# Instance normalisation: tiles of one row per partition in twelve buffers instead of two rows in six

## The chip, the cores and the metric

The kernel runs on one core of one Trainium2 chip. The metric is the device time of one execution in microseconds, from the first to the last instruction, as the median of several runs. The engines that matter are VectorE (DVE in the profile), which computes statistics, ScalarE (ACT), which applies a scale and a bias to every element and also issues the stores, SyncE (SP), which issues the loads, and the core's 16 DMA engines, which carry both.

## The reference

The input is 256 x 256 rows of 4096 floats (1073.74 MB), and the output has the same size. Each row is normalised by its own mean and variance.

```python
def setup_inputs():
    batch, channels, length = 256, 256, 4096
    return {"x": np.random.randn(batch, channels, length).astype(np.float32),
            "eps": np.float32(1e-5)}

def reference(x, eps):
    mean = np.mean(x, axis=2, keepdims=True)
    var = np.var(x, axis=2, keepdims=True)
    return ((x - mean) / np.sqrt(var + eps)).astype(np.float32)
```

All data must be read once and written once; a row of 16 KB fits into one partition of on-chip memory.

## The kernel before

A tile is 128 partitions x 2 rows x 4096 floats, 4 MB, so there are 256 tiles. Each partition's two rows lie next to each other in memory, 32 KB in one piece. Six such tiles fit at once. For every tile, SyncE issues the load. VectorE computes partial statistics of 512 elements each (eight per row), combines them (`bn_aggr`) to mean and variance. ScalarE takes the square root, VectorE the reciprocal and the bias -mean x rstd. ScalarE then normalises each row in place and issues the store from the same buffer.

```python
    P = 128
    K = 2
    BUFS = 6
    # ...
    x_t = x_flat.rearrange("(t p k) d -> t p k d", p=P, k=K)
    out_t = out_flat.rearrange("(t p k) d -> t p k d", p=P, k=K)
    # ... nsub = 8
    io = ctx.enter_context(tc.tile_pool(name="io", bufs=BUFS))
    small = ctx.enter_context(tc.tile_pool(name="small", bufs=2 * BUFS))
    # ...
    for i in range(ntiles):
        x_tile = io.tile([P, K, d], mybir.dt.float32)
        nc.sync.dma_start(out=x_tile, in_=x_t[i])

        # ... stats, mv, rstd, nbias from the small pool
        for r in range(K):
            for j in range(nsub):
                nc.vector.bn_stats(out=stats[:, r, j, :], in_=xr[:, r, j, :])
            nc.vector.bn_aggr(out=mv[:, r, :], in_=stats[:, r])

        nc.scalar.activation(out=rstd, in_=mv[:, :, 1], func=Sqrt, bias=eps_tile, scale=1.0)  # shortened
        nc.vector.reciprocal(out=rstd, in_=rstd)
        nc.vector.scalar_tensor_tensor(out=nbias, in0=mv[:, :, 0], scalar=-1.0, in1=rstd, ...)

        for r in range(K):
            nc.scalar.activation(out=x_tile[:, r, :], in_=x_tile[:, r, :], func=Identity,
                                 bias=nbias[:, r : r + 1], scale=rstd[:, r : r + 1])  # shortened
        nc.scalar.dma_start(out=out_t[i], in_=x_tile)
```

The order in which an engine executes is not that of the source. When the program is built, a scheduler decides for each engine in which order its instructions stand, and inserts the waits; on the chip every engine then works strictly in that order. The pools give out buffers in turn: a load into a buffer waits until the store that last read it has landed.

Of the kernel before, what the change touches and what calls it, by code (L numbers as in the profile page):

```python
# [1 line left out]

# [4 lines left out]


@with_exitstack  # L10
def kernel(
    ctx: ExitStack,
    tc: tile.TileContext,
    x: bass.AP,
    eps: bass.AP,
    out: bass.AP,
):
    nc = tc.nc
    P = 128
    K = 2  # L20
    BUFS = 6

    x_flat = x.flatten_outer_dims()
    out_flat = out.flatten_outer_dims()
    n, d = x_flat.shape
    rows_per_tile = P * K
    assert n % rows_per_tile == 0
    ntiles = n // rows_per_tile

    x_t = x_flat.rearrange("(t p k) d -> t p k d", p=P, k=K)  # L30
    out_t = out_flat.rearrange("(t p k) d -> t p k d", p=P, k=K)

    BN_FMAX = nc.vector.BN_STATS_FMAX
    nsub = (d + BN_FMAX - 1) // BN_FMAX
    assert d % BN_FMAX == 0

    io = ctx.enter_context(tc.tile_pool(name="io", bufs=BUFS))
    small = ctx.enter_context(tc.tile_pool(name="small", bufs=2 * BUFS))
    singles = ctx.enter_context(tc.tile_pool(name="singles", bufs=1))

    eps_tile = singles.tile([P, 1], mybir.dt.float32)
    nc.vector.memset(eps_tile, eps)  # L42

    for i in range(ntiles):
        x_tile = io.tile([P, K, d], mybir.dt.float32)
        nc.sync.dma_start(out=x_tile, in_=x_t[i])  # L46

        stats = small.tile([P, K, nsub, 6], mybir.dt.float32)
        mv = small.tile([P, K, 2], mybir.dt.float32)
        rstd = small.tile([P, K], mybir.dt.float32)  # L50
        nbias = small.tile([P, K], mybir.dt.float32)
        xr = x_tile.rearrange("p k (s f) -> p k s f", s=nsub)
        for r in range(K):
            for j in range(nsub):
                nc.vector.bn_stats(out=stats[:, r, j, :], in_=xr[:, r, j, :])  # L55
            nc.vector.bn_aggr(out=mv[:, r, :], in_=stats[:, r])  # L56

        nc.scalar.activation(  # L58
            out=rstd,
            in_=mv[:, :, 1],  # L60
            func=mybir.ActivationFunctionType.Sqrt,
            bias=eps_tile,
            scale=1.0,
        )
        nc.vector.reciprocal(out=rstd, in_=rstd)  # L65

        nc.vector.scalar_tensor_tensor(  # L67
            out=nbias,
            in0=mv[:, :, 0],
            scalar=-1.0,  # L70
            in1=rstd,
            op0=mybir.AluOpType.mult,
            op1=mybir.AluOpType.mult,
        )

        for r in range(K):
            nc.scalar.activation(  # L77
                out=x_tile[:, r, :],
                in_=x_tile[:, r, :],
                func=mybir.ActivationFunctionType.Identity,  # L80
                bias=nbias[:, r : r + 1],
                scale=rstd[:, r : r + 1],
            )
        nc.scalar.dma_start(out=out_t[i], in_=x_tile)


# [1 line left out]
_INS = ['x', 'eps']  # L88
_OUTS = [((256, 256, 4096), 'float32')]
#: Inputs that are plain numbers.  # L90
_NUMBERS = {'eps': 9.999999747378752e-06}


# [26 lines left out]
```

## Time and profile before

| | |
|---|---|
| time, median of 3 | 5180.87 us (5179.3 to 5187.54) |
| read + written | 1073.74 MB + 1073.74 MB |
| VectorE: partial statistics | 4096 of 674 ns, 2464.1 us |
| VectorE: combining | 512 of 363 ns, 185.7 us |
| ScalarE: normalising a row | 512 of 3793 ns, 1917.8 us |
| ScalarE: square root | 256 of 280 ns, 71.7 us |
| VectorE: reciprocal, bias | 256 each, 27.7 and 41.0 us |
| loads | 256 of 4096 KB, median 23.7 us from issue to landing |
| stores | 256 of 4096 KB, median 18.6 us from issue to landing |

The profile page gives each engine's busy time; its table of queues says how much of the 16 DMA engines' time the packets of each queue took. A further view lists who waited for whom; there the queue of SyncE (SPq) shows what each load had to wait for before it was issued. The chain that ended last goes back from the last instruction, at each step to what released it. Windows give busy time and moved bytes of a stretch. Below the page, the trace holds a record of every DMA packet with its start, duration, size and queue.

### The profile page before, as it was taken

How to read it: one execution, taken by the hardware profiler on the slowest of the kernel's cores; microseconds unless marked ns; L12 is line 12 of the kernel's file. 1: busy time of each engine (PE TensorE's matmuls, PEld its weight loads, DVE VectorE, ACT ScalarE, POOL GpSimd, SP SyncE). 2: the span in 40 equal slices, each digit the busy share in tenths (PEclk: the TensorE clock that was granted, in tenths of full speed). 3: DMA queues.
4: the chain of work that ended last, by engine and by line, in shares of the span. 5: the costliest groups of instructions: out<-in, count | busy, mean ns of one | idle time of the engine just before them, and what ended most of it. 6: DMA issues, size and time to landing. Idle time of an engine off the chain costs nothing.

```text
span 5180.7 us, 7450 instructions
## 1 busy us (share of the span) xinstructions
DVE 2654.0 (51%) x5121; ACT 1967.0 (38%) x769; POOL 0.2 (0%) x4
## 2 busy tenths in 40 slices
DVE  6544555554455555444555554455555445555543
ACT  3333333433333433433343433333343333334334
POOL 0000000000000000000000000000000000000000
DMA  9999999999999999999999999999999999999998
GB/s 425 412 410 413 420 417 422 417 414 416 410 416 413 417 418 414 413 412 417 417 416 418 413 414 418 410 417 420 417 415 417 417 413 417 417 419 415 415 416 367
DMA packets 73786, 2147.99 MB, mean 415 GB/s; under 512 B 8192, under 2 KB 8192, under 8 KB 8192
## 3 DMA queue, kind: packets, MB, share of 16 engines
q1 hardware_dynamic: 36864, 1073.76, 49.7%
q10 hardware_dynamic: 36864, 1073.76, 49.5%
q14 instruction: 58, 0.48, 0.0%
HBM read 1073.74 MB, written 1073.74 MB: 415 GB/s over the span
## 4 chain that ended last, share of the span: by engine, by line
DMA 69%; DVE 17%; ACT 7%; issue 6%; another core or an unknown queue 0%; SPq 0%
DMA x_tile<-in_x_dram 43%; DMA out_dram<-x_tile 26%; DVE stats L55 16%; ACT x_tile L77 7%; DVE mv L56 1%; DVE nbias L67 0%; SPq L46 0%; DVE rstd L65 0%; ACT rstd L58 0%
## 5 line engine op out<-in xcount | busy, mean ns | idle before, releaser
L55 DVE BATCH_NORM_STATS2 stats<-x_tile 128x6 f32<-128x512 f32 x4096 | 2464.1, 674 | 2460.3 <-DMA x_tile<-in_x_dram 2460.3
L77 ACT ACTIVATE x_tile<-x_tile,nbias,rstd 128x4096 f32<-128x4096 f32 x512 | 1917.8, 3793 | 3172.3 <-DVE nbias L67 3172.3
L56 DVE BATCH_NORM_AGGREGATE mv<-stats 128x2 f32<-128x48 f32 x512 | 185.7, 363 | 8.8
L58 ACT ACTIVATE rstd<-mv,eps_tile 128x2 f32<-128x2 f32 x256 | 71.7, 280 | 23.9 <-DVE mv L56 23.9
L67 DVE SCALAR_TENSOR_TENSOR nbias<-mv,rstd 128x2 f32<-128x2 f32 x256 | 41.0, 160 | 8.8
L65 DVE RECIPROCAL rstd<-rstd 128x2 f32<-128x2 f32 x256 | 27.7, 108 | 23.6 <-ACT rstd L58 23.6
L58 ACT ACT_TABLE_LOAD x1 | 1.3, 1283 | 0.7 <-PEq L101 0.7
L42 DVE MEMSET eps_tile<- 128x1 f32 x1 | 0.1, 59 | 0.8 <-PEq L101 0.8
L101 POOL MEMSET const-bfloat16-1.0<- 128x1 bf16 x1 | 0.1, 101 | 0.0
L101 POOL MEMSET const-uint8-127<- 128x1 uint8 x1 | 0.1, 101 | 0.0
L101 POOL MEMSET const-float32-0.0<- 128x1 f32 x1 | 0.1, 98 | 0.2 <-issue 0.2
L101 POOL MEMSET const-float32-1.0<- 128x1 f32 x1 | 0.1, 98 | 0.0
## 6 DMA issues: line engine op xcount, KB each, us to landing
x_tile<-in_x_dram SPq DMA_DIRECT2D x256, 4096.0 KB, 23.7
out_dram<-x_tile ACTq DMA_DIRECT2D x256, 4096.0 KB, 18.6
```

What stands on the lines that cost most here:

```text
L42: nc.vector.memset(eps_tile, eps)
L55: nc.vector.bn_stats(out=stats[:, r, j, :], in_=xr[:, r, j, :])
L56: nc.vector.bn_aggr(out=mv[:, r, :], in_=stats[:, r])
L58: nc.scalar.activation(out=rstd, in_=mv[:, :, 1], func=mybir.ActivationFunctionType.Sqrt, bias=eps_tile, scale=1.0,)
L65: nc.vector.reciprocal(out=rstd, in_=rstd)
L67: nc.vector.scalar_tensor_tensor(out=nbias, in0=mv[:, :, 0], scalar=-1.0, in1=rstd, op0=mybir.AluOpType.mult, op1=mybir.AluOpType.mult,)
L77: nc.scalar.activation(out=x_tile[:, r, :], in_=x_tile[:, r, :], func=mybir.ActivationFunctionType.Identity, bias=nbias[:, r : r + 1], sca ...
L101: nc = _bacc.Bacc("TRN2", target_bir_lowering=False, num_devices=1)
```

## The change

A tile becomes one row per partition, 2 MB, and there are twelve of them, so the same memory is split in smaller pieces. The loop in the source now issues seven loads ahead of the first tile's computation, and later load i + 7 behind tile i. The small tiles (statistics, mean and variance, reciprocal, bias) are for one row, and their pool has eight buffers of each instead of twelve. Loads stay on SyncE's queue and stores on ScalarE's. The purpose is a finer pipeline: a tile is computed and stored after half as much data has landed, a buffer comes free in smaller steps, and filling and draining at both ends are shorter.

```diff
-    K = 2
-    BUFS = 6
+    K = 1
+    BUFS = 12
+    AHEAD = 7
 ...
-    small = ctx.enter_context(tc.tile_pool(name="small", bufs=2 * BUFS))
+    small = ctx.enter_context(tc.tile_pool(name="small", bufs=8))
 ...
-    for i in range(ntiles):
+    tiles = {}
+
+    def load(i):
         x_tile = io.tile([P, K, d], mybir.dt.float32)
         nc.sync.dma_start(out=x_tile, in_=x_t[i])
+        tiles[i] = x_tile
 
-        stats = small.tile([P, K, nsub, 6], mybir.dt.float32)
-        mv = small.tile([P, K, 2], mybir.dt.float32)
-        rstd = small.tile([P, K], mybir.dt.float32)
-        nbias = small.tile([P, K], mybir.dt.float32)
+    def row(x_tile, r):
+        stats = small.tile([P, nsub, 6], mybir.dt.float32)
+        mv = small.tile([P, 2], mybir.dt.float32)
+        rstd = small.tile([P, 1], mybir.dt.float32)
+        nbias = small.tile([P, 1], mybir.dt.float32)
 ... (the same operations, for one row)
+    def finish(i):
+        x_tile = tiles.pop(i)
         for r in range(K):
+            row(x_tile, r)
         nc.scalar.dma_start(out=out_t[i], in_=x_tile)
+
+    for i in range(AHEAD):
+        load(i)
+    for i in range(ntiles):
+        finish(i)
+        if i + AHEAD < ntiles:
+            load(i + AHEAD)
```

More of the change, by code (lines that the diff above doesn't have):

```diff
@@ L25 @@
     n, d = x_flat.shape
-    rows_per_tile = P * K
-    assert n % rows_per_tile == 0
-    ntiles = n // rows_per_tile
+    ntiles = n // (P * K)
+    assert n == ntiles * P * K
     x_t = x_flat.rearrange("(t p k) d -> t p k d", p=P, k=K)
     out_t = out_flat.rearrange("(t p k) d -> t p k d", p=P, k=K)
-    BN_FMAX = nc.vector.BN_STATS_FMAX
-    nsub = (d + BN_FMAX - 1) // BN_FMAX
-    assert d % BN_FMAX == 0
+    FMAX = nc.vector.BN_STATS_FMAX
+    nsub = d // FMAX
+    assert d == nsub * FMAX
     io = ctx.enter_context(tc.tile_pool(name="io", bufs=BUFS))
-    small = ctx.enter_context(tc.tile_pool(name="small", bufs=2 * BUFS))
+    small = ctx.enter_context(tc.tile_pool(name="small", bufs=8))
     singles = ctx.enter_context(tc.tile_pool(name="singles", bufs=1))
@@ L42 @@
     nc.vector.memset(eps_tile, eps)
-    for i in range(ntiles):
+    tiles = {}
+    def load(i):
         x_tile = io.tile([P, K, d], mybir.dt.float32)
         nc.sync.dma_start(out=x_tile, in_=x_t[i])
-        stats = small.tile([P, K, nsub, 6], mybir.dt.float32)
-        mv = small.tile([P, K, 2], mybir.dt.float32)
-        rstd = small.tile([P, K], mybir.dt.float32)
-        nbias = small.tile([P, K], mybir.dt.float32)
+        tiles[i] = x_tile
+    def row(x_tile, r):
         xr = x_tile.rearrange("p k (s f) -> p k s f", s=nsub)
[L53 to L56, printed above, removed]
+        stats = small.tile([P, nsub, 6], mybir.dt.float32)
+        mv = small.tile([P, 2], mybir.dt.float32)
+        rstd = small.tile([P, 1], mybir.dt.float32)
+        nbias = small.tile([P, 1], mybir.dt.float32)
+        for j in range(nsub):
+            nc.vector.bn_stats(out=stats[:, j, :], in_=xr[:, r, j, :])
+        nc.vector.bn_aggr(out=mv, in_=stats)
         nc.scalar.activation(
             out=rstd,
-            in_=mv[:, :, 1],
+            in_=mv[:, 1:2],
             func=mybir.ActivationFunctionType.Sqrt,
@@ L68 @@
             out=nbias,
-            in0=mv[:, :, 0],
+            in0=mv[:, 0:1],
             scalar=-1.0,
@@ L74 @@
         )
-        for r in range(K):
[L77 to L83, printed above, removed]
-        nc.scalar.dma_start(out=out_t[i], in_=x_tile)
+        nc.scalar.activation(
+            out=x_tile[:, r, :],
+            in_=x_tile[:, r, :],
+            func=mybir.ActivationFunctionType.Identity,
+            bias=nbias,
+            scale=rstd,
+        )
+    def finish(i):
+        x_tile = tiles.pop(i)
+        for r in range(K):
+            row(x_tile, r)
+        nc.scalar.dma_start(out=out_t[i], in_=x_tile)
+    for i in range(AHEAD):
[4 more added lines that the diff above has]
+            load(i + AHEAD)
 _INS = ['x', 'eps']
```

## The prediction

> **What bounds the kernel now.** I read the page first: engines, slices, queues.
>
> ```profile
> DVE 2654.0 (51%) x5121; ACT 1967.0 (38%) x769; POOL 0.2 (0%) x4
> ...
> DMA packets 73786, 2147.99 MB, mean 415 GB/s; under 512 B 8192, under 2 KB 8192, under 8 KB 8192
> ...
> q1 hardware_dynamic: 36864, 1073.76, 49.7%
> q10 hardware_dynamic: 36864, 1073.76, 49.5%
> ```
>
> VectorE (DVE) and ScalarE (ACT) are half idle; the two queues of transfers (q1 loads, q10 stores) together fill 99.2% of the 16 DMA engines. So the transfers are the bound, and the first question is what fills those 99.2%. The trace's packet records answer it. There are 65,536 packets of 32 KB (8 per engine and transfer) and 8,192 of 4 bytes (one completion per engine and transfer, 9 ns). The median 32 KB packet takes 1213 ns, which is 432 GB/s over 16 engines. At that pace all of them would take 4096 per engine x 1.213 = 4968 us. The time that packets take above 1213 ns adds up to 164 us per engine, completions to 4.6 us. The remaining 44 us the engines stand empty. So 5181 = 4968 + 164 + 5 + 44; only some 210 us are not plain transfer.
>
> Next I asked where those 164 us lie, by windows (columns: busy time of DVE, ACT, POOL, clock, DMA share, GB/s).
>
> ```profile
> 50.00:110.00 60.00, 31.50 (x60) 15.35 (x6) 0.00 (x0) 1.00 1.01 436
> ...
> 2557.00:2563.00 6.00, 1.70 (x5) 4.20 (x2) 0.00 (x0) 1.00 0.99 350
> ```
>
> Near the start, loads and stores are both queued all the time, packets alternate, and the rate is full. In mid-run one queue runs empty for 8 to 12 us at a time; when it fills again all 16 engines stall together (the second window: 350 GB/s). Grouping the long packets by time, the 140 places where a load joins after a stores-only stretch cost 0.63 us each, 88 us in all; 45 where a store joins after loads only cost 0.40 us.
>
> Why does a queue run empty? The waits of SyncE's queue (us in total, times, longest) and the chain in order of time (start, us, what) say so.
>
> ```profile
> SPq L46 <- DMA out_dram<-x_tile: 4914.6, 248, 33.2
> ```
>
> ```profile
> 2554.49 26.10 DMA x_tile<-in_x_dram
> ...
> 2580.61 5.43 DVE stats L55 x9
> ...
> 2594.79 3.79 ACT x_tile L77
> 2598.57 0.03 ACT rstd L58
> 2598.60 16.70 DMA out_dram<-x_tile
> ...
> 2615.43 25.72 DMA x_tile<-in_x_dram
> ```
>
> Nearly every load waits for a store to free its buffer. The chain is a loop: a load lands (26.1 us), statistics and normalising follow (18.0), the store (16.7), and its buffer starts a load again after 60.9 us. Three tiles come per loop (60.7 x 256/3 = 5180). But there are six buffers. The other three are hidden in the order that the scheduler gave VectorE (tile names are numbered, 30 per tile here; `rstd_4960` belongs to `stats_4958`):
>
> ```
> before   BNStats x16 + Aggregate  mv_5049 <- stats_5048      (tile k)
>          Reciprocal               rstd_4960                  (tile k-3)
>          TensorScalarPtr          nbias_4961                 (tile k-3)
> ```
>
> Reciprocal and bias of a tile stand behind the statistics of the third tile after it. A tile has its statistics as soon as it lands, then lies for three tiles. So what normalises after the landing at 2580.6 is the tile three earlier, and only 6 - 3 = 3 buffers circulate among load, compute and store. A loop has 3 x 8 x 2 x 1.213 = 58.2 us of transfer per engine; the rest up to 60.7 are stalls (164/85.3 loops = 1.92) and gaps of about 0.3.
>
> **What the Trainium skill says.** DMA: Bandwidth & Descriptors, section Where 436 GB/s comes from: 16 ports of 32 B at 850 MHz, 435 GB/s. The trace agrees: 432 within packets. Same page, Why small descriptors are slow: about 3 cycles fixed per packet, 3.5 ns at that clock as an estimate. The trace has more: 64 instruction-fetch packets of 8 KB take 309 ns, 32 KB take 1213, and the line through both leaves 7.7 ns per packet. I use the trace's. Same page, Anatomy of one DMA: DMA engines don't wait on semaphores; the wait is at the issuing sequencer. The SyncE row above agrees, and it is why a load held for a buffer leaves its queue empty. Same page, Latency and other measured facts: HBM access takes 0.2 us, 2 us at high load. The stalls lie between; that they are such a latency is an inference, but it suggests a stall of fixed time rather than one proportional to packet size.
>
> **The change part by part.**
>
> 1. *Packets.* 16 KB per partition instead of 32: on the line above 309 + 8192/24576 x 904 = 610 ns, so 8192 per engine x 0.6103 = 5000 us, +31 us. Completions double to 16,384, 9 us: +5.
> 2. *Issues.* 512 of each: SyncE has nothing else to do; ScalarE pays 256 more issues of 0.34 us and 256 more square roots of 0.28 us, 159 us on an engine that is 38% busy. Hidden.
> 3. *VectorE.* Reciprocals and biases double in number: 27.7 + 41.0 = 69 us more, at 51% load. Hidden. Neither engine becomes the bound: 10 us of transfer per tile against 5.5 and 4.4 us.
> 4. *Buffers.* 12 x 2 MB are the same bytes as 6 x 4 MB. But the built order has changed (20 per tile number):
>
> ```
> after    BNStats x8               stats_4080                 (tile k)
>          Reciprocal               rstd_3902                  (tile k-9)
>          TensorScalarPtr          nbias_3903                 (tile k-9)
>          BNStatsAggregate         mv_4061 <- stats_4060      (tile k-1)
> ```
>
> A tile now lies for nine tiles. The lag is 1 at the start, reaches 9 at about tile 25 and stays there; an aggregate of tile k-1 right behind the bias of tile k-9 is just what the small pool's eight buffers allow. AHEAD = 7 orders the source, but what holds a load is its buffer. So 12 - 9 = 3 buffers circulate again, of half the size: 6 MB in motion each way instead of 12.
> 5. *The loop.* Three 2 MB tiles carry 3 x 8 x 2 x 0.6103 = 29.3 us of transfer. Without sharing, the chain of one tile would be: compute 4.8 (eight statistics of 0.6) + 0.4 + 3.8 = 9.1; store 4.9 + 1.4; load 4.9 + 2.6 (the fastest of before landed in 11.1 and 12.3 us, where 4 MB alone take 9.7): 23 us. That is under 29, so the engines stay mostly filled, with less slack than before (41 under 58). There are 512/3 = 171 loops instead of 85, each with its queue changes. If a change costs what it cost, that is 1.92 + 0.3 us per loop. About 163 loops run with the full lag: 163 x 1.92 = 313 us of stalls, 49 us of gaps.
> 6. *Ends.* The start is 2 us. After the last load has landed the engines stand nearly empty while one tile is computed: the window 5121.6 to 5140 moved 85 GB/s, 14.8 us lost. Half the tile, half of that: 8 us.
>
> Sum: 5000 + 9 + 313 + 49 + 10 = **5381 us**, rounded to 5380: 3.8% slower.
>
> **Rivals.**
>
> *Steady mixing.* Smaller tiles with twelve buffers keep both queues filled, as in the window 50 to 110. The stalls vanish: 5000 + 9 + 15 = about 5025 us, 3% faster. This is what the change is for, and the packet count alone forbids more. It needs some 8 or more free buffers; the lag of nine is fixed in VectorE's order, which runs in order, so I give it little.
>
> *Stalls shrink with the tile.* If a stall is so many packets and not so many microseconds, 164 us stay in all, and gaps too: 5000 + 9 + 164 + 25 + 10 = 5208 us, "same". For it: I have not shown what a stall is. Against: they come when a queue refills, whatever lay in it before, and at 0.2 to 0.7 us they are shorter than a packet.
>
> *The loop gets bound by latency.* 23 us unshared in 29 leave 6 us of slack, and the tiles share the engines. If an average of 2 us per loop more stand empty, that is 326 us: 5700 us. For it: the gap of before came although there were 17 us of slack. Against: the loop is self-spacing; a tile that finds the engines empty catches up.
>
> *Fixed cost per transfer.* 512 transfers more could each add a microsecond or two. Before's 512 transfers together have only 208 us of stall and gap, and overlapped ones near the start cost none, so it isn't the transfer but the empty queue.
>
> **Range and chances.** The centre rests on a fixed stall per loop. The lower end, 5220, is the second rival; the upper, 5560, is half of the third's extra idle time. 2% slower begins at 5284; stalls must shrink by about a third to come below it: 0.80 slower, 0.16 within 2%, 0.04 faster.
>
> **What would show it.** Median 16 KB packet near 610 ns; a nine-tile distance between statistics and normalising; SyncE still waiting mostly for stores; stalls of 300 us and more in the long packets, at about 170 x 2; DMA share a little below before's, some 400 GB/s. Median landing should fall to about half, 10 to 14 us. I'm wrong if SyncE waits for loads instead (four in flight; then mixing holds), if packets of 16 KB take much more than 610 ns, or if the engines stand empty for several us per loop.

## The result and the profile after

The changed kernel takes 5574.64 us (5569.64 to 5577.5) beside 5180.09 us of the kernel before: a ratio of 1.0737, 95% interval 1.0695 to 1.078. The prediction said 5380 us, range 5220 to 5560: the right direction, and about half of the loss.

The page of the changed kernel, the lines that answer to those shown of before: busy engines, packets, the two queues.

```profile
DVE 2784.0 (50%) x5633; ACT 2041.7 (37%) x1025; POOL 0.2 (0%) x4
...
DMA packets 147528, 2148.14 MB, mean 385 GB/s; under 512 B 16384, under 2 KB 16384, under 8 KB 16384
...
q1 hardware_dynamic: 73728, 1073.77, 49.4%
q10 hardware_dynamic: 73728, 1073.77, 47.8%
```

The compute engines are as idle as before. The same bytes move at 385 GB/s instead of 415, although packets still fill 97.2% of the DMA engines' time: most of what was lost is lost inside packets that take too long. Two windows show the extremes (busy time of DVE, ACT, POOL, clock, DMA share, GB/s).

```profile
2794.00:2797.00 3.00, 1.00 (x2) 2.04 (x2) 0.00 (x0) 1.00 0.34 142
50.00:110.00 60.00, 38.45 (x75) 15.94 (x8) 0.00 (x0) 1.00 1.01 432
```

Near the start the small tiles run at full rate; in mid-run there are stretches in which the engines stand nearly empty. What SyncE's queue waited for (us in total, times, longest) has not changed its nature:

```profile
SPq L48 <- DMA out_dram<-x_tile: 5209.1, 493, 15.9
SPq L48 <- DMA x_tile<-in_x_dram: 92.2, 12, 9.4
```

The landing of a store ended 493 of these waits. The chain in order of time (start, us, what), from one load to the load into the buffer that it frees:

```profile
2758.45 13.96 DMA x_tile<-in_x_dram
...
2772.43 4.85 DVE stats L58 x8
...
2781.28 0.12 ACT rstd L60
2781.40 14.75 DMA out_dram<-x_tile
...
2796.20 11.97 DMA x_tile<-in_x_dram
```

Load 14.0, compute 9.0, store 14.8: this loop took 37.8 us; over the middle half of the run the mean is 3 x 10.93 = 32.8 us for three tiles, whose transfer needs 29.4. What is normalised behind a landing is a tile that had landed about 99 us earlier: in the records tile 250 has its last statistics at 2668.9 and its bias at 2767.8, nine tiles of 11 us.

From the packet records, us per DMA engine. "Rest" is the span less the other columns. It is too low by what neighbouring packets overlap in the records, a few ns each, which shows where it is small or negative. The last column is the share of time in which packets of only one of the two queues were being moved.

| | packets at their median | completions | stalls (time above the median) | rest (empty) | span | one queue only |
|---|---|---|---|---|---|---|
| before | 4968 | 5 | 164 | 44 | 5181 | 52% |
| predicted | 5000 | 9 | 313 | 59 | 5381 | |
| after | 5005 | 9 | 405 | 154 | 5573 | 59% |

The packets cost what was predicted (median 611 ns). Stalls are 92 us more, empty time 95 us more, packets 5 us: together the 192 us between 5381 and the profiled run.

### The profile page after: what moved, and what is told of

It reads as the page before. It is cut to its first block, busy times and chain, and to the rows that moved or that the text cites. A ratio compares the mean times of both kernels' runs of the same rounds, so it can differ in the third digit from the quotient of the medians.

```text
span 5572.9 us, 9236 instructions
## 1 busy us (share of the span) xinstructions
DVE 2784.0 (50%) x5633; ACT 2041.7 (37%) x1025; POOL 0.2 (0%) x4
## 4 chain that ended last, share of the span: by engine, by line
DMA 72%; DVE 16%; issue 12%; ACT 1%; SPq 0%
DMA x_tile<-in_x_dram 40%; DMA out_dram<-x_tile 31%; DVE stats L58 15%; DVE nbias L68 1%; ACT rstd L60 0%; ACT x_tile L76 0%; DVE rstd L67 0%; SPq L48 0%; DVE mv L59 0%
## 5 line engine op out<-in xcount | busy, mean ns | idle before, releaser
L76 ACT ACTIVATE x_tile<-x_tile,nbias,rstd 128x4096 f32<-128x4096 f32 x512 | 1945.5, 3800 | 3505.5 <-DVE nbias L68 3505.5
L60 ACT ACTIVATE rstd<-mv,eps_tile 128x1 f32<-128x1 f32 x512 | 142.7, 279 | 13.4 <-DVE mv L59 13.4
L67 DVE RECIPROCAL rstd<-rstd 128x1 f32<-128x1 f32 x512 | 74.8, 146 | 36.0 <-ACT rstd L60 36.0
L68 DVE SCALAR_TENSOR_TENSOR nbias<-mv,rstd 128x1 f32<-128x1 f32 x512 | 81.4, 159 | 17.1
## 6 DMA issues: line engine op xcount, KB each, us to landing
out_dram<-x_tile ACTq DMA_DIRECT2D x512, 2048.0 KB, 11.9
```

The lines of the kernel that those rows point to most:

```text
L60: nc.scalar.activation(out=rstd, in_=mv[:, 1:2], func=mybir.ActivationFunctionType.Sqrt, bias=eps_tile, scale=1.0,)
L68: nc.vector.scalar_tensor_tensor(out=nbias, in0=mv[:, 0:1], scalar=-1.0, in1=rstd, op0=mybir.AluOpType.mult, op1=mybir.AluOpType.mult,)
```

## The experiments

The lag of a kernel is how many tiles later, in VectorE's order, a tile's reciprocal and bias stand behind its own statistics. The tiles in motion (those that circulate) are the large buffers less the lag. Two questions: is it the lag that costs the time, and why did three circulating tiles of half the size lose more than a doubled number of the old losses?

### The lag against the size of the transfers

Two edits change the pools alone. The lag then found in the built order of VectorE, in tiles: 9 with eight small buffers, 7 with four, 3 with two, 1 with one; with six or ten small buffers it is 9 as well. With six 2 MB buffers and two small ones it is 3.

```diff
# lag 1 (first) and lag 7 (second), on the changed kernel
-    small = ctx.enter_context(tc.tile_pool(name="small", bufs=8))
+    small = ctx.enter_context(tc.tile_pool(name="small", bufs=1))
+    small = ctx.enter_context(tc.tile_pool(name="small", bufs=4))
```

Lag 1. 

> The changed kernel with one buffer instead of eight in the small pool; in the built order a tile's reciprocal then stands behind the statistics of the next tile (lag 1 instead of 9), so 11 tiles of 2 MB circulate. Lag theory: both queues stay filled, stalls under 50 us and gaps under 30 us, time 5010 to 5060 us. Rival, that 512 transfers of 2 MB in 16 KB packets are dearer in themselves: about 5575 us as before the edit.

Measured 5028.64 us in the median, ratio to before 0.9696 (0.9678 to 0.9715). A run more than 1.5% above the fastest of its kernel is left out of the ratios; here that is one of four, which took 5154.16 us beside 5028.34 to 5028.64. It is the one with a profile. Its rate in 40 slices of the span:

```profile
GB/s 421 431 431 431 431 431 431 431 431 431 431 431 431 431 431 431 431 431 431 431 428 423 429 426 429 427 428 410 380 374 374 374 372 375 371 404 431 431 431 350
```

It starts at 431 GB/s, and for seven slices late in the run it moves only 371 to 380. There, from 3750 to 4500 us, 15 of a transfer's 16 completions come within 1 us and the last one 32 us after them. What makes one DMA engine's share come so late isn't shown, nor why it costs time here: with lag 3 and twelve buffers (below) a load's last completion comes 14 us after the others in the second half of the run, and the rate stays at 424 GB/s or more until the last slice. This loss is a second one, apart from the lag.

Lag 7. 

> The changed kernel with four small buffers: lag 7, so 5 tiles of 2 MB circulate. Lag theory: 5 tiles carry 49 us of transfer against an unshared chain of 23 us; the queues run empty more seldom, 5080 to 5250 us. Rival, transfer size: 5575 us.

Measured 5035.02 us, 0.9708 (0.9693 to 0.9724): better than the 5080 that I allowed at best.

Six buffers instead of twelve:

```diff
-    BUFS = 12
+    BUFS = 6
-    small = ctx.enter_context(tc.tile_pool(name="small", bufs=8))
+    small = ctx.enter_context(tc.tile_pool(name="small", bufs=2))
```

> The changed kernel with six 2 MB buffers (12 MB) instead of twelve and two small buffers; lag 3, so 6 - 3 = 3 tiles circulate, as 12 - 9 = 3 do in the changed kernel. Lag theory: half the memory, the same time, 5575 us within 2%. Rival, that the memory given to the tiles decides: slower by 5% or more, about 5900 us.

Measured 5593.53 us, 1.0786 (1.0766 to 1.0807). The page, queues and rate of this kernel:

```profile
DMA packets 147532, 2148.17 MB, mean 385 GB/s; under 512 B 16384, under 2 KB 16384, under 8 KB 16384
...
q1 hardware_dynamic: 73728, 1073.77, 49.5%
q10 hardware_dynamic: 73728, 1073.77, 47.8%
```

Line for line the changed kernel: 12 - 9 and 6 - 3 are the same three tiles in motion, and the other 12 MB of the changed kernel only hold tiles that wait for their reciprocal. With the same 512 transfers and 16 KB packets, lag 7 and lag 1 are 10% faster than lag 9. So 2 MB transfers aren't dear in themselves. They are dear when the lag leaves only three of them in motion.

### How many tiles have to circulate

```diff
# 4 circulating: seven buffers, lag 3
-    BUFS = 12
+    BUFS = 7
-    small = ctx.enter_context(tc.tile_pool(name="small", bufs=8))
+    small = ctx.enter_context(tc.tile_pool(name="small", bufs=2))
```

> The changed kernel with seven 2 MB buffers and two small ones: lag 3, 4 tiles circulate, 39 us of transfer against an unshared chain of 23 us. Slack theory: between 3 tiles (5575) and 5 tiles (5035), nearer to 5, about 5080 to 5200 us. Fixed sum per loop: 512/4 = 128 loops of 3.2 us lost give 5014 + 410 = about 5420 us.

Measured 5033.22 us, 0.9679 (0.9628 to 0.9731). Both expectations were too high: one tile more than three takes away everything. The page of this kernel and a window of its mid-run:

```profile
DMA packets 147532, 2148.17 MB, mean 427 GB/s; under 512 B 16384, under 2 KB 16384, under 8 KB 16384
```

```profile
2500.00:2600.00 100.00, 55.51 (x112) 40.10 (x22) 0.00 (x0) 1.00 1.01 429
```

Lag 3 with all twelve buffers (two small ones, nothing else changed), nine tiles in motion:

> The changed kernel with two buffers in the small pool: lag 3, 9 tiles of 2 MB circulate. Lag theory: as with lag 7 and lag 1, 5025 to 5040 us; nothing more to gain once the queues stay filled. Rival: time goes on falling with each further circulating tile, below 5020 us.

Measured 5028.51 us, 0.9669 (0.9618 to 0.972): flat from four tiles on. Its four runs lie close together (5028.27 to 5028.85), and it beats both kernels: by 3.3% the one before, by 9.8% the changed one (5574.64 against 5028.51). It differs from the changed kernel in one number. The packet records of both:

| | stalls | rest | one queue only |
|---|---|---|---|
| 4 circulate | 40 | -23 | 7% |
| 9 circulate | 25 | -12 | 3% |

### Why three tiles lose so much

ScalarE normalises half a row, so the compute part of the chain is shorter; lag 9 and three tiles in motion stay. The output's second halves are the unchanged input.

```diff
-            out=x_tile[:, r, :],
-            in_=x_tile[:, r, :],
+            out=x_tile[:, r, : d // 2],
+            in_=x_tile[:, r, : d // 2],
```

> The changed kernel with ScalarE normalising only the first 2048 of each row's 4096 elements (the rest is stored as it was loaded). Lag 9 and 3 circulating tiles stay; in the built order the reciprocal moves up behind two statistics of the later tile, so the compute part of the chain falls from 9.1 to about 4 us and the unshared chain from 23 to 18 us, both under the 29 us of transfer of three tiles. If stalls and gaps are a fixed sum per loop (step 5 of the prediction): 5575 us within 1%. Rival, that the loop was mis-sized because its chain stands too near the 29 us (slack): clearly faster, 5150 to 5450 us.

Measured 5151.58 us, 0.9896 (0.9832 to 0.9961) of before, 423 us less than the changed kernel. Both chains without sharing, 23 and 18 us, are below 29 us, and yet stalls fall from 405 to 153 us and the rest from 154 to -14. A fixed sum per loop is refuted: what a loop loses depends on how long its compute part is. The busy engines, the packets and the issues of this kernel's page:

```profile
DVE 2667.5 (52%) x5633; ACT 1168.3 (23%) x1025; POOL 0.2 (0%) x4
...
DMA packets 147528, 2148.14 MB, mean 417 GB/s; under 512 B 16384, under 2 KB 16384, under 8 KB 16384
...
x_tile<-in_x_dram SPq DMA_DIRECT2D x512, 2048.0 KB, 13.2
out_dram<-x_tile ACTq DMA_DIRECT2D x512, 2048.0 KB, 13.0
```

ScalarE was nowhere near a bound in the changed kernel (37%), yet halving its work, together with the reciprocal that the scheduler then places earlier, is worth nearly 8%: both stood in the chain that frees buffers. How the gain divides between the two wasn't tried.

From this a rule for the loop, to be tested on the kernel before. If both queues are to stay filled, a load and a store move at half the rate each. The chain has to be counted with that, not as if a tile had the engines to itself. The kernel before with the same halving of the normalising (here too the reciprocal moves up in VectorE's order, behind the first of the later tile's two rows):

> The kernel before (4 MB tiles, six buffers, lag 3, 3 circulating) with ScalarE normalising only the first half of each row. The compute part of the chain falls from 18 to about 10 us. Theory after the runs so far: three tiles keep both queues filled only if compute plus a load and a store that share the engines fit into the transfer of three tiles. For 4 MB that is 58 us, a shared load and store are 2 x 19.4 plus some 2.5 us each to the first packet, 44 us, so compute may take up to about 14 us: 18 doesn't fit, 10 does, and nearly all stalls vanish: 4990 to 5040 us. Rival, a fixed sum of stalls and gaps per loop (step 5 of the prediction): 5180 us.

Measured 5028.03 us, 0.9666 (0.9631 to 0.9701), inside the 4990 to 5040 that the rule gave and 3% under the 5180 of a fixed sum: stalls 57 us instead of 164, one queue alone in 17% of the time instead of 52%. Its page:

```profile
DVE 2641.6 (53%) x5121; ACT 1093.5 (22%) x769; POOL 0.2 (0%) x4
...
DMA packets 73786, 2147.99 MB, mean 427 GB/s; under 512 B 8192, under 2 KB 8192, under 8 KB 8192
...
x_tile<-in_x_dram SPq DMA_DIRECT2D x256, 4096.0 KB, 24.2
out_dram<-x_tile ACTq DMA_DIRECT2D x256, 4096.0 KB, 24.1
```

The loop of before closes in the time of its transfers, 24.2 + 24.1 + 10 = 58.3 us, as soon as compute leaves room for a load and a store at half rate.

### Packets by themselves

The kernel before, its two rows of a partition now 2 MB apart, so that every transfer has 256 packets of 16 KB:

```diff
-    x_t = x_flat.rearrange("(t p k) d -> t p k d", p=P, k=K)
-    out_t = out_flat.rearrange("(t p k) d -> t p k d", p=P, k=K)
+    x_t = x_flat.rearrange("(t k p) d -> t p k d", p=P, k=K)
+    out_t = out_flat.rearrange("(t k p) d -> t p k d", p=P, k=K)
```

> The kernel before with its 4 MB tiles, six buffers and lag 3, but the two rows of a partition 2 MB apart in memory, so each transfer has 256 packets of 16 KB instead of 128 of 32 KB. Packet cost alone, stalls unchanged: 5181 + 31 = 5212 us, 5190 to 5240. Rival, that a stall or gap goes with the packets (their number doubles): 5340 us or more.

Measured 5181.28 us, 0.9971 (0.9951 to 0.9991). The packets' medians add up to 5005 us instead of 4968 (611 ns each), the stalls stay at 163, but the rest falls from 44 to 10 us, and nothing of the 37 us reaches the time. Neither expectation held: stalls don't go with the number of packets, and the packet cost doesn't show in the time. Where the 37 us went isn't shown. One queue is alone in 37% of the time instead of 52%, but the time in which no packet moves at all is 29 us beside 27. Part of the 37 may be bookkeeping: with four tiles in motion, 16 KB packets at their median, stalls and completions add up to 23 us more than the span, so neighbouring records overlap.

### 4 MB tiles without the lag

The kernel before with one small buffer instead of twelve (lag 1, five tiles in motion):

```diff
-    small = ctx.enter_context(tc.tile_pool(name="small", bufs=2 * BUFS))
+    small = ctx.enter_context(tc.tile_pool(name="small", bufs=1))
```

> The kernel before with one buffer in the small pool: lag 1 instead of 3, so 5 tiles of 4 MB circulate instead of 3. Lag theory: 4968 us of packets + 5 + about 20 to 40 at the ends and in stalls: 4995 to 5030 us, faster than both kernels. Rival, that the 164 us of stalls belong to the mixing of reads and writes and not to the waits for buffers: 5180 us.

Measured 5118.62 us in the median, but its runs spread from 5012.33 to 5210.43, and the ratio, 0.9721 (0.9652 to 0.9789), rests on the two quicker ones, 5012.33 and 5070.08. The profiled run (span 5208.7 us) moves 433 GB/s at first and 399 later on; in its later half 15 of the 16 DMA engines finish a load within 1 us of each other and the last one 23 us after them, as in the long run with lag 1 above. What makes it fall behind stays open.

The changed kernel's code with 4 MB tiles, rows computed one by one:

```diff
-    K = 1
-    BUFS = 12
-    AHEAD = 7
+    K = 2
+    BUFS = 6
+    AHEAD = 4
-    small = ctx.enter_context(tc.tile_pool(name="small", bufs=8))
+    small = ctx.enter_context(tc.tile_pool(name="small", bufs=2))
```

> The changed kernel's code (rows computed one by one) with 4 MB tiles of two rows in six buffers and two small buffers: the lag is 2 to 3 rows, one to one and a half tiles, so more than 4 tiles of 4 MB circulate, in 32 KB packets. Lag theory: 4968 + 5 + 20 to 40 = 4990 to 5020 us, the fastest form. Rival: 4 MB with few tiles loses its even mixing during the run, as the lag-1 form of the kernel before did in some runs: 5050 to 5200 us.

Measured 5029.25 us (5018.57 to 5050.39), 0.966 (0.9619 to 0.9701): between the two expectations. Its profiled run, the longest, keeps 73 us of stalls, and the form doesn't beat the 2 MB form by the 37 us that its larger packets save.

## Why the prediction was right and wrong

**What bounds the kernel** was right: transfers, with the loss in stalls where an empty queue refills. Where both stay filled (four tiles and more, or less compute in the chain) stalls are 25 to 73 us in all. Three profiles stand outside this: the changed kernel with half the normalising (153), and the two runs in which one DMA engine fell behind (97 with lag 1, 174 with 4 MB tiles and lag 1).

**Part 1, packets**, was right in their duration: 611 ns and 5005 us against 610 and 5000. That a change of packets alone would show in the time was not: on the kernel before it was absorbed.

**Parts 2 and 3, issues and VectorE**, were right in what they conclude: ScalarE is 37% and VectorE 50% busy, neither a bound. Reciprocals and biases took 88 us more instead of 69.

**Part 4, buffers**, was right and decided the direction: 12 - 9 = 3 tiles in motion. Six buffers with lag 3 gave the same time, and a lag of 7 turned 5575 into 5035. Its aside that the lag of nine is just what the eight small buffers allow was wrong: six or ten of them give nine too. The twelve large buffers less three look like the ceiling (six less three before); that is read from the built orders, not from the scheduler.

**Part 5, the loop**, failed, and in one step: "Without sharing, the chain of one tile would be ... 23 us. That is under 29, so the engines stay mostly filled", and, built on it, "If a change costs what it cost, that is 1.92 + 0.3 us per loop." The comparison has to be made with sharing. Half rate makes a 2 MB load or store 9.8 us. With some 2.5 us to the first packet (an estimate from the fastest load of before, 12.3 us where 9.7 are transfer; used for the store too, where the prediction had 1.4, which would make each chain about 1 us shorter), the chain is 9.1 + 2 x 12.3 = 34 us, over the 29.4 of three tiles. By this count it can't close with both queues filled, so now and then a transfer must run alone at full rate, and queues empty and refill. Measured: 32.8 us per loop, one queue alone in 59% of the time. The same count sorts the other kernels, except that the changed kernel with half the normalising, at the margin, still loses some:

| | compute + shared load and store, us | transfer of the tiles in motion, us | span over packets and completions, us |
|---|---|---|---|
| after, 3 tiles | 9 + 25 = 34 | 29 | 559 |
| before, 3 tiles | 18 + 44 = 62 | 58 | 208 |
| after, half normalising | 4 + 25 = 29 | 29 | 139 |
| before, half normalising | 10 + 44 = 54 | 58 | 57 |
| 2 MB, 4 tiles | 9 + 25 = 34 | 39 | 18 |

The two runs in which one DMA engine fell behind, and the 4 MB form with rows computed one by one (76 us), lose more than this count says; it doesn't cover that loss.

The cost of a change was no constant either. Grouped as before, the 215 places where a store joins after loads only cost 0.76 us each (0.40 before, 45 places), and 190 where loads follow alone on stores cost 0.83. The total per loop with full lag came to 405/163 = 2.5 us of stalls and 0.9 us empty, instead of 1.92 and 0.3. The signs that the prediction named did appear (611 ns, a distance of nine tiles, waits for stores, stalls over 300 us, landings of 13.0 and 11.9 us), but none of them separates a fixed loss per loop from a loop that is too long for its tiles.

**Part 6, the ends**, was not separated by a run. The window from 5512 to 5530 after the last load still moved 305 GB/s, where before's moved 85, so the end lost less than the 8 us assumed: 18 x (1 - 305/432) = 5 us.

**The rivals.** Steady mixing was refused for the right reason, and its 5025 us is what the kernel reaches once the lag is gone (5028). The loop bound by latency, given 5700 us and half of it for the upper end, was the nearest: it named the right cause, but expected the loss as 2 us more of empty engines per loop, where 0.6 were added and the rest lay in stalls. Its objection that the loop is self-spacing is what the runs refute. Stalls that shrink with the tile (164 us in all) are refuted by the 405, and a fixed cost per transfer by 5028 us with the same 512 transfers each way. That a stall is of fixed time was argued from a latency; the runs only show that it doesn't go with the number of packets.

## What to carry to other kernels

Count the buffers that really move: those of the pool less those that a scheduler's order holds between two operations on the same tile; the built order shows it, the source doesn't. Then compare the loop of one buffer, with load and store at the rate they have when both directions are busy, with the transfer time of the tiles in motion; if it doesn't fit, an engine that is 60% idle costs time. Here one tile more in motion, or a smaller scratch pool (two small buffers instead of eight), was worth 10%; cutting tiles finer at the same lag-bound count only halved what was in flight.

## What had not been expected

- The step from three to four tiles in motion is a cliff: 5593 to 5033 us, with nothing left for five, nine or eleven (5035, 5029, 5029 in the median; one of the four runs with eleven took 5154).
- Fewer small buffers are faster: eight give 5575 us, four 5035, two 5029. Up to the ceiling of nine, the scratch pool sets how far VectorE is ordered ahead.
- Reads and writes mixed packet by packet lose next to nothing: 429 GB/s in mid-run with four tiles, and a 16 KB packet's median of 611 ns is 429 GB/s over 16 engines.
- 16 KB packets in place of 32 KB, 37 us of DMA engine time more by their medians, left the kernel before's time within 0.3%.
